# A two-block transformer kernel: the depthwise convolution moves to TensorE, two kinds of narrow products stand in unbroken groups, and the first output projection takes its K-tiles in another order

## The chip, the cores and the metric

The kernel runs on one core of one Trainium2 chip. A core has five engines, each with its own queue of instructions in order: TensorE (PE, with weight loads listed apart as PEld), VectorE (DVE), ScalarE (ACT), GpSimd (POOL) and SyncE (SP), which here issues nearly all DMAs. The metric is device time in microseconds (us), lower is better.

## The reference, cut to what matters

Two blocks work on x of 512 positions by 1024 channels, all in float32. The parts that the change touches:

```python
# first block, mixer: attention over 8 heads of 64, beside a depthwise convolution of 31 taps
q, k, v, f_logit, conv_val, conv_gate = split(h @ w_in)
attn = softmax(q k^T / 8 + cum[t] - cum[s], causal) @ v
u = conv_val * sigmoid(conv_gate)                       # 512 positions x 512 channels
u = sum over d of w[30 - d, c] * u[t - d, c] + b        # 31 taps
u = silu(layer_norm(u))
y = concat([attn, u]) @ w_o                             # K = 1024, then SwiGLU
# second block, state-space mixer: 32 heads of 64, four chunks of 128 positions
y_diag[c] = (scores * exp(seg)) @ xdt                   # 128x128 by 128x64 for each head and chunk
# second block, stick-breaking attention over 16 heads of 64
a = ...;  o = a @ v
```

## The kernel before, in words

The kernel is one program of four stages, *fox* (the first mixer), *ffn*, *mamba* and *sb* (stick-breaking), each with a projection in, its own work and an output projection. Positions are cut into four tiles of 128.

**Projections.** A float32 weight is split into a high part (`whi`, ACT, L268) and a rest (`wlo`, DVE or POOL, L272), and each projection product is three matmuls of 128x512 (L327 to L329). Weights come through a ring of four raw buffers (`load`, L240), which SP fills in the order of a plan (L246). In the plan stand also the tiles of the `ada_w` matrices; DVE sums those up (L498) between other work, and they take the same raw buffers.

**Order of work.** `run` (L184) lays lists of steps beside each other, and a scheduler then sets each engine's order by priorities (the table `PRIO`, L33: a higher number draws a step forward), by dependencies and by its own idea of when an operand is ready. On the chip each engine keeps that order: an instruction that waits holds up all behind it.

**Convolution** (`conv`, L851). A tile `ct` of 128 channels lies with channels in partitions and positions along the row. Tap d adds the row, moved by d, times one weight per channel: one instruction on DVE (L867) for tiles 1 and 2, two (ACT L870, POOL L871) for tiles 3 and 0; tap 0 is an ACT instruction (L865). The table `TAPS` (L52) says how many taps go beside each part of the stage. The taps end during the third attention head pair; then come the layer norm's steps (`ln`, L1025).

**Products with v** (`pv`, L761, used four times in fox and eight times in sb, a pair of heads each time). For each tile s of keys and each head e, the probabilities are transposed (L772), copied from PSUM (L774; ACT for e = 0, DVE for e = 1) and multiplied with v (L780). The product is 64 columns wide; head e writes the half of the PSUM partitions that begins at 64e. A row of the order names a whole product; TensorE runs a float32 product as two instructions, and so the trace counts two for each.

**State-space diagonals** (`diag`, L1262). For each of four groups and four chunks, 16 products of 64x64 (L1267) take the decayed scores that `decay` (L1234, ends with DVE L1244) makes head by head.

**Output projection** (`Out`, L79). `w_o` has eight K-tiles: 0 to 3 are attention's, 4 to 7 the convolution's; they are taken in this order. The last attention pair and the layer norm (L1035) stand between the third and the fourth K-tile.

Of the kernel before, what the change touches and what calls it, by code (L numbers as in the profile page):

```python
# [8 lines left out]
F32 = mybir.dt.float32  # L9
# [7 lines left out]
P = 128  # L17
# [14 lines left out]
NTAP = (30, 30, 0, 0)  # L32
PRIO = {  # L33
    "attend": 15, "attend_last": 190, "ba": 100, "bb": -800, "bc": 200, "bd": 100, "be": 25, "bf": -770, "bl":
    -400, "bn": 90, "bp": -200, "br": -5, "bt": -50, "chain": 100, "colsum": 50, "conv.evac": 20, "conv.fin": 200,
    "conv.split": 0, "conv.sum": -100, "conv.tap": -800, "decay": -860, "erows": 190, "evac": -390, "evac_t": 430,
# [9 lines left out]
    "mamba.sum": -410, "mod": -55, "norm": 50, "off": -10, "osplit": -100, "rows": 200, "sb.evac": 400, "sb.fin":  # L46
# [4 lines left out]

TAPS = (4, 9, 11, 4, 5, 4, 1, 2, 8, 3, 8, 13, 0, 5, 7, 7, 8, 18, 11, 0, 6, 0, 0, 0, 0, 0)  # L52
# [81 lines left out]
class Body:  # L134
# [281 lines left out]
    def consts(self):  # L416
# [25 lines left out]
                                compare_op=ALU.is_ge, fill=0.0)  # L442

# [317 lines left out]
    def pv(self, Ps, v, c0, done, tag="pa"):  # L761

        nc = self.nc
        box, pts = {}, {}

        def trans(s, e):
            if s == 0 and e == 0:
                box["po"] = self.psum(tag)
# [4 lines left out]
            pts[s, e] = self.w512()  # L773
            (nc.scalar.copy, nc.vector.tensor_copy)[e](pts[s, e][:, :N], ps[:, :N])  # L774

        def mms(s):

            for e in (0, 1):
                c = c0 + 64 * e
                nc.tensor.matmul(box["po"][64 * e : 64 * e + 64, s * P :], lhsT=v[:, s, c : c + 64],  # L780
                                 rhs=pts[s, e][:, : S - s * P], start=s == 0, stop=s == NT - 1)

        steps = []
        for i in range(8 + LAG):
            def f(i=i):
                if i < 8:
                    trans(i // 2, i % 2)
                if i >= LAG and (i - LAG) % 2:
                    mms((i - LAG) // 2)
            steps.append(f)  # L790
        return steps + [lambda: done(box["po"])]


    def fox(self):
# [45 lines left out]
        out = Out(self, A["w_o"][0], list(range(8)),  # L840
# [4 lines left out]
        taps, ptaps = [], []  # L845
# [4 lines left out]

        def conv(ct, val, sg):  # L851
            u = us[:, ct, :]
            nc.vector.tensor_tensor(u, val, sg, ALU.mult)  # L853

            def tap(d):
                wc = self.conv_w[:, (30 - d) * 4 + ct : (30 - d) * 4 + ct + 1]
                acc = yc[:, ct, d:]

                def f():
                    with self.prio("tap"):  # L860
                        g()

                def g():
                    if d == 0:
                        nc.scalar.activation(acc, u, AF.Identity, scale=wc, bias=self.v_conv_b[:, ct : ct + 1])  # L865
                    elif d <= NTAP[ct - 1]:
                        nc.vector.scalar_tensor_tensor(acc, u[:, : S - d], wc, acc, ALU.mult, ALU.add)  # L867
                    else:
                        p = self.w512()[:, : S - d]
                        nc.scalar.mul(p, u[:, : S - d], wc)  # L870
                        nc.gpsimd.tensor_tensor(acc, acc, p, ALU.add)  # L871
                return f

            tap(0)()
            return [tap(d) for d in range(1, 31)]

        def some(l, n):
            r, l[:n] = l[:n], []
            return r
# [6 lines left out]
        for k in range(KD):  # L886
            wh, wl = self.take(cu[k])
            self.drop(cu[k])
            if k == KD - 1:
                yc, us = self.big(), self.big()  # L890
                y.append(yc)
# [796 lines left out]
```

## Time and profile before

| | |
|---|---|
| time, three runs | 1434.6, 1439.05, 1439.44 us (median 1439.05) |
| profiled execution | 1434.7 us, span 1432.9 us |
| busy PE, PEld | 1328.3 us (93%), 1024.1 us (71%) |
| busy DVE, ACT, POOL | 953.5 us (67%), 699.6 us (49%), 418.5 us (29%) |
| mean granted TensorE clock | 0.974 of full speed |
| chain that ended last | PE 58%, DVE 18%, issue 7%, POOL 7%, ACT 6%, DMA 2% |

How to read it: busy time is a share of the whole span, but the stages differ. In fox (about the first 300 us) DVE is the fullest engine and PE has gaps; from 340 us on PE is nearly full. The granted clock has two levels, 2.4 GHz (1.0) and 1.2 GHz (0.5); a stretch between them was partly at either. Matmuls overlap, so one matmul's cost is the time from its start to the next one's start, not its listed duration.

### The profile page before, as it was taken

How to read it: one execution, taken by the hardware profiler on the slowest of the kernel's cores; microseconds unless marked ns; L12 is line 12 of the kernel's file. 1: busy time of each engine (PE TensorE's matmuls, PEld its weight loads, DVE VectorE, ACT ScalarE, POOL GpSimd, SP SyncE). 2: the span in 40 equal slices, each digit the busy share in tenths (PEclk: the TensorE clock that was granted, in tenths of full speed). 3: DMA queues.
4: the chain of work that ended last, by engine and by line, in shares of the span. 5: the costliest groups of instructions: out<-in, count | busy, mean ns of one | idle time of the engine just before them, and what ended most of it. 6: DMA issues, size and time to landing. Idle time of an engine off the chain costs nothing.

```text
span 1432.9 us, 19210 instructions
## 1 busy us (share of the span) xinstructions
PE 1328.3 (93%) x7175; PEld 1024.1 (71%) x7175; DVE 953.5 (67%) x1328; ACT 699.6 (49%) x1278; POOL 418.5 (29%) x370
## 2 busy tenths in 40 slices
PE   7895678999999999999899999999999999999897
PEld 5664454777888888888677777787787877566556
DVE  7999998565455454413878978587629428676854
ACT  5463556554222224313768475767426336554633
POOL 3565697214000000000203452544002003353531
PEclk9997799999999999999999999999999999999999
DMA  9553653014376664323357464231243524222101
GB/s 312 163 167 101 204 176 117 21 28 154 120 230 219 191 187 136 96 96 107 88 170 252 145 186 143 86 129 56 74 131 121 175 89 133 61 73 74 59 1 59
DMA packets 126680, 183.76 MB, mean 128 GB/s; under 512 B 8764, under 2 KB 90068, under 8 KB 125564
## 3 DMA queue, kind: packets, MB, share of 16 engines
q1 hardware_dynamic: 126540, 182.54, 40.8%
q8 instruction: 56, 0.92, 0.3%
q14 instruction: 36, 0.29, 0.1%
q10 hardware_dynamic: 48, 0.01, 0.0%
HBM read 174.05 MB, written 2.18 MB: 123 GB/s over the span
## 4 chain that ended last, share of the span: by engine, by line
PE 58%; DVE 18%; issue 7%; POOL 7%; ACT 6%; DMA 2%; SPq 0%; ACTq 0%; DVEq 0%; POOLq 0%
PE pa L329 14%; PE pa L328 13%; PE pa L327 13%; DVE b L867 4%; POOL w L1418 3%; PE ps L328 3%; PE ps L329 3%; PE ps L327 3%; DVE wlo L272 3%; PE pa L780 2%; DVE acc L498 2%; PE ps L772 1%; POOL w L1216 1%; ACT whi L268 1%; DVE w L1416 1%
## 5 line engine op out<-in xcount | busy, mean ns | idle before, releaser
L272 DVE TENSOR_TENSOR wlo<-raw,whi 128x1024 fp32r<-128x1024 f32 (+1 forms) x161 | 208.1, 1303 | 203.6 <-ACT whi L268 202.0
L268 ACT CAST whi<-raw 128x1024 fp32r<-128x1024 f32 (+1 forms) x177 | 183.1, 1046 | 298.1 <-PE pa L328 121.8
L327 PE MATMUL pa<-b,whi 128*128 128x512 f32 x744 | 298.5, 401 | 0.0
L328 PE MATMUL pa<-b,whi 128*128 128x512 f32 x744 | 297.6, 400 | 0.0
L329 PE MATMUL pa<-b,wlo 128*128 128x512 f32 x744 | 297.1, 399 | 0.0
L498 DVE SCALAR_TENSOR_TENSOR acc<-raw,c,acc 128x1024 f32<-128x1024 f32 x84 | 126.3, 1504 | 64.9 <-DMA raw<-in_ada_w_dram 38.9
L327 PE MATMUL pa<-whi,b 128*128 128x512 f32 x424 | 166.8, 395 | 2.8 <-DVE b L853 2.8
L674 POOL TENSOR_TENSOR b<-w,b 128x512 fp32r<-128x512 f32 x24 | 39.3, 1651 | 441.5 <-DVE sm L579 287.8
L329 PEld LDWEIGHTS pa<-b,wlo 128*128 128x128 f32 x744 | 140.7, 189 | 38.4 <-issue 9.5
L328 PE MATMUL pa<-wlo,b 128*128 128x512 f32 x424 | 167.3, 395 | 0.3 <-DVE wlo L272 0.3
L329 PE MATMUL pa<-whi,b 128*128 128x512 f32 x424 | 166.8, 395 | 0.0
L328 PEld LDWEIGHTS pa<-b,whi 128*128 128x128 f32 x744 | 141.4, 190 | 32.6 <-issue 6.1
L327 PEld LDWEIGHTS pa<-b,whi 128*128 128x128 f32 x744 | 140.8, 189 | 31.6 <-issue 4.3
L871 POOL TENSOR_TENSOR b<-b,w 128x511 f32<-128x511 f32 (+29 forms) x60 | 94.1, 1589 | 30.0 <-ACT w L870 28.7
L327 PEld LDWEIGHTS pa<-whi,b 128*128 128x128 f32 x424 | 80.0, 189 | 20.7 <-DVE b L853 4.0
L328 PEld LDWEIGHTS pa<-wlo,b 128*128 128x128 f32 x424 | 80.1, 189 | 17.2 <-DVE wlo L272 1.0
L329 PEld LDWEIGHTS pa<-whi,b 128*128 128x128 f32 x424 | 80.0, 189 | 16.2
L1418 POOL TENSOR_TENSOR w<-w,w 128x127 f32<-128x127 f32 (+3 forms) x64 | 80.8, 1265 | 16.4 <-DVE w L1416 15.2
L772 PE MATMUL ps<-ident,w 128*128 128x128 f32 x240 | 53.2, 295 | 24.3 <-POOL w L1419 12.1
L867 DVE SCALAR_TENSOR_TENSOR b<-b,cw,b 128x511 f32<-128x511 f32 (+29 forms) x60 | 73.4, 1258 | 0.1
L327 PE MATMUL ps<-whi,b 128*128 128x512 f32 x184 | 72.2, 392 | 0.0
L328 PE MATMUL ps<-wlo,b 128*128 128x512 f32 x184 | 72.1, 392 | 0.0
(352 smaller groups left out, 2345.2 us busy)
## 6 DMA issues: line engine op xcount, KB each, us to landing
raw<-in_ada_w_dram SPq DMA_DIRECT2D x80, 512.0 KB, 3.9
raw<-in_w_ffn_in_dram SPq DMA_DIRECT2D x44, 512.0 KB, 4.6
raw<-in_m_in_w_dram SPq DMA_DIRECT2D x40, 512.0 KB, 3.7
raw<-in_w_ffn_out_dram SPq DMA_DIRECT2D x22, 512.0 KB, 4.1
b<-in_ada_w_dram SPq DMA_DIRECT2D x16, 512.0 KB, 7.8
raw<-in_kv_ada_w_dram SPq DMA_DIRECT2D x16, 512.0 KB, 4.8
b<-cumd SPq DMA_DIRECT2D x8, 1024.0 KB, 6.6
raw<-in_m_out_w_dram SPq DMA_DIRECT2D x16, 512.0 KB, 4.4
```

Source lines behind the costliest of these rows:

```text
L268: nc.scalar.copy(hi[:, :n], u.raw)
L272: eng.tensor_tensor(lo[:, :n], u.raw, hi[:, :n].bitcast(F32), ALU.subtract)
L327: mm(ps, lhsT=lh, rhs=rh, start=first, stop=False)
L328: mm(ps, lhsT=lh, rhs=rl, start=False, stop=False)
L329: mm(ps, lhsT=ll, rhs=rh, start=False, stop=last)
L498: nc.vector.scalar_tensor_tensor(acc, raw, ck, acc, ALU.mult, ALU.add)
L674: nc.gpsimd.tensor_tensor(lo, y[i], hi.bitcast(F32), ALU.subtract)
L772: nc.tensor.transpose(ps[:, (t - s) * P : (t - s + 1) * P], Ps()[e][t][:, s * P : (s + 1) * P], self.ident)
L780: nc.tensor.matmul(box["po"][64 * e : 64 * e + 64, s * P :], lhsT=v[:, s, c : c + 64], rhs=pts[s, e][:, : S - s * P], start=s == 0, stop=s ...
L867: nc.vector.scalar_tensor_tensor(acc, u[:, : S - d], wc, acc, ALU.mult, ALU.add)
L871: nc.gpsimd.tensor_tensor(acc, acc, p, ALU.add)
L1418: nc.gpsimd.tensor_tensor(pr_[:, : N - 1], pr_[:, : N - 1], R[:, 1:N], ALU.mult)
```

## The change

Three things are edited.

1. **Convolution.** The tap tables go. `u` of a channel tile is stored to a DRAM tile that has four zeros in front, and loaded back four times, one, two, three and four places moved, into a tile `u4` with 32 channels by 4 moves in the partitions and four channel groups side by side. Products of 128 rows by 32 columns with `taps` (diagonal matrices that POOL makes from the weights) then add up all taps: 8 steps of four moves, four channel groups in four column quarters, so 32 products for a channel tile and 128 in all. The layer norm runs beside the second projection pair. At the start the conv weights are loaded in another layout by eight DMAs, and four DMAs write the zeros.
2. **Groups.** `pv` issues the products of key tiles 0 and 1 as one group and of 2 and 3 as another; `diag` issues a chunk's 16 as one. The first product of a group waits for what the others need as well, and a high priority (3000, also under the names `pv` and `diag_mm` in `PRIO`) keeps a group together.
3. **Output projection of fox.** K-tiles 4 to 7 come first, and the last attention pair runs beside output steps.

```diff
-LAG = 4
+LAG = 2
...
-    -400, "bn": 90, "bp": -200, "br": -5, "bt": -50, "chain": 100, "colsum": 50, "conv.evac": 20, "conv.fin": 200,
+    -400, "bn": 90, "bp": -200, "br": -5, "bt": -50, "chain": 100, "colsum": 50, "conv_mm": 3000, "conv.evac": 20, "conv.fin": 200,
...
+    def wait(self, i, prev):
+        self.tc.add_manual_dep(i, prev.name, mybir.DependencyInfo(
+            mybir.DependencyClass.Sync, mybir.DependencyReason.DATA), reason="wait")
...
     def pv(self, Ps, v, c0, done, tag="pa"):
...
+            if s < 2:
+                pts[s, e] = self.w512()[:, :N]
+            elif e == 0:
+                two = self.w512()
+                pts[s, 0], pts[s, 1] = two[:, :N], two[:, N : 2 * N]
+            copies[s, e] = (nc.scalar.copy, nc.vector.tensor_copy)[e](pts[s, e], ps[:, :N])
+        def mms(*ss):
+            if 0 in ss:
+                box["po"] = self.psum(tag)
+            with self.prio("pv"):
+                for s in ss:
+                    for e in (0, 1):
...
+                        if s == ss[0] and e == 0:
+                            for k in ((s, 1), (ss[1], 0), (ss[1], 1)):
+                                self.wait(m.ins, copies[k].ins)
+        steps = [lambda s=s, e=e: trans(s, e) for s in range(NT) for e in (0, 1)]
+        steps.insert(4 + LAG, lambda: mms(0, 1))
+        return steps + [lambda: None] * LAG + [lambda: mms(2, 3), lambda: done(box["po"])]
...
-        out = Out(self, A["w_o"][0], list(range(8)),
+        out = Out(self, A["w_o"][0], [4, 5, 6, 7, 0, 1, 2, 3],
...
         def conv(ct, val, sg):
+            u = self.w512()
             nc.vector.tensor_tensor(u, val, sg, ALU.mult)
+            nc.sync.dma_start(ud[ct][:, 4:], u)
+            u4 = self.big()
+            loads = [nc.sync.dma_start(u4[32 * s : 32 * s + 32, :, :],
+                                       ud[ct][:, 1 + s : 1 + s + S].rearrange("(g c) x -> c g x", g=4))
+                     for s in range(4)]
+            def products():
+                ps = self.psum()
+                with self.prio("conv_mm"):
+                    for m in range(8):
+                        for g in range(4):
+                            i = nc.tensor.matmul(ps[32 * g : 32 * g + 32, 4 * m :], lhsT=taps[ct // 2][:, ct % 2, 7 - m, g, :],
+                                                 rhs=u4[:, g, : S - 4 * m], start=m == 0, stop=m == 7)
+                            if m == g == 0:
+                                for l in loads:
+                                    self.wait(i.ins, l.ins)
+                nc.scalar.activation(yc[:, ct, :], ps, AF.Identity, bias=self.v_conv_b[:, ct : ct + 1])
...
-        self.run(pv, some(taps, TAPS[2]), some(ptaps, TAPS[3]))
+        self.run(pv[:8])
+        self.run(pv[8:], tp[:3])
...
+            self.run(main[2 * i], self.at("attend", attend(i - 1)) if i else self.at("ln", ln[:6]))
+            self.run(main[2 * i + 1], self.at("scores", scores(i)) + idle, self.at("ln", ln[6:]) if i == 0 else [])
+        self.run(out.steps((0, 1), (0, 1)), self.at("attend_last", attend(2, "ps")))
+        self.run(out.steps((0, 1), (2, 3)), self.at("scores_last", scores(3)) + idle)
+        self.run(out.steps((0, 1), (4, 5)), self.at("attend_last", attend(3, "ps")))
+        self.run(out.steps((2, 3), range(4)))
...
             def diag(c):
...
+                with self.prio("diag_mm"):
...
+                            if i == t == 0 and c == 0:
+                                self.wait(m.ins, box["decayed"].ins)
...
+        for i in range(8):
+            s0 = int(i == 0)
+            nc.sync.dma_start(sw[16 * i : 16 * i + 16, 32 * s0 : P].rearrange("g (s c) -> g s c", c=32),
+                              A["conv_w"][0][4 * i + s0 - 1 : 4 * i + 3, :].rearrange("s (g c) -> g s c", c=32))
+        for u in self.u_pads:
+            nc.sync.dma_start(u, sw[:, P:])
```

On PE in fox, at the end of the value projection, the program before goes from that projection to the gate's 32-column products (L373):

```order
L327 MATMUL pa_991<-whi_968,b_91 128x512
L328 MATMUL pa_991<-wlo_969,b_91 128x512
L329 MATMUL pa_991<-whi_968,b_93 128x512
L373 MATMUL pa_1123<-b_90,whi_999 32x512 x4
L373 MATMUL pa_1123<-b_92,whi_999 32x512 x4
L373 MATMUL pa_1123<-b_91,whi_999 32x512 x4
L373 MATMUL pa_1123<-b_93,whi_999 32x512 x4
```

At the same place the changed program has the convolution's products (L882), of three channel tiles one after the other:

```order
L328 MATMUL pa_989<-whi_1063,b_91 128x512
L329 MATMUL pa_989<-wlo_1064,b_91 128x512
L330 MATMUL pa_989<-whi_1063,b_93 128x512
L473 MATMUL ps_942<-ident,w_888 128x96
L882 MATMUL ps_1014<-b_840,b_872 32x512 x4
L882 MATMUL ps_1014<-b_840,b_872 32x508 x4
L882 MATMUL ps_1014<-b_840,b_872 32x504 x4
L882 MATMUL ps_1014<-b_840,b_872 32x500 x4
```

So 96 products stand ahead of the gate's products there; those of channel tile 0 come right behind them.

On PE in sb, at the first `pv` of that stage, the program before has the products (L780) one or two at a time, between projection matmuls (L327 to L329), transposes (L772) and scores (L749, L754):

```order
L780 MATMUL pa_10244<-w_10250,b_9420 64x512
L328 MATMUL pa_10252<-b_9936,whi_10045 128x512
L780 MATMUL pa_10244<-w_10261,b_9420 64x512
L329 MATMUL pa_10252<-b_9935,wlo_10046 128x512
L327 MATMUL pa_10348<-b_9850,whi_10083 128x512
L772 MATMUL ps_10308<-ident,w_10137 128x128
L328 MATMUL pa_10348<-b_9851,whi_10083 128x512
L780 MATMUL pa_10244<-w_10270,b_9420 64x384
L329 MATMUL pa_10348<-b_9850,wlo_10084 128x512
L749 MATMUL ps_10352<-b_10096 128x128
L780 MATMUL pa_10244<-w_10281,b_9420 64x384
L780 MATMUL pa_10244<-w_10289,b_9420 64x256
```

In the changed program (products L793, transposes L777) the first group stands so:

```order
L777 MATMUL ps_10225<-ident,w_10073 128x128
L329 MATMUL pa_10191<-b_9876,whi_9985 128x512
L777 MATMUL ps_10230<-ident,w_10074 128x128
L777 MATMUL ps_10225<-ident,w_10076 128x128
L793 MATMUL pa_10237<-w_10189,b_9360 64x512
L793 MATMUL pa_10237<-w_10200,b_9360 64x512
L793 MATMUL pa_10237<-w_10209,b_9360 64x384
L793 MATMUL pa_10237<-w_10220,b_9360 64x384
L777 MATMUL ps_10230<-ident,w_10077 128x128
L330 MATMUL pa_10191<-b_9875,wlo_9986 128x512
```

The four products of key tiles 0 and 1 are together and stand ahead of the last transposes; those of tiles 2 and 3 follow as a second group, 11 rows further on.

On SP in fox, the changed program's stores and loads of `u` (L871, L873) stand ahead of the weight loads (L247) that follow the value projection's; the program before has no such rows.

```order
L247 DMA raw_987<-in_ada_w_dram 128x1024
L871 DMA u_95<-w_837 128x512
L467 DMA w_878<-in_conv_ln_g_dram 4x128
L467 DMA w_878<-in_conv_ln_b_dram 4x128
L467 DMA w_878<-in_m_conv_b_dram 24x128
L467 DMA w_878<-in_c_dram 8x128
L873 DMA b_840<-u_95 32x4x512 x4
L871 DMA u_96<-w_849 128x512
```

Each set of four loads waits for its own store; three more such sets follow before SP is past them.

## Rows read from the trace of the kernel before

**Rows 1.** Stretches: us, busy PE, PEld, DVE, ACT, POOL; clock, DMA, GB/s.

```profile
71.40:157.00 85.60, 59.37 (x322) 43.61 (x320) 82.38 (x86) 37.93 (x57) 43.91 (x28) 0.84 0.49 150
157.00:267.00 110.00, 93.96 (x537) 62.05 (x537) 96.88 (x117) 71.11 (x152) 83.49 (x48) 0.92 0.45 139
...
1210.00:1360.00 150.00, 134.58 (x617) 90.28 (x616) 111.33 (x129) 82.37 (x174) 69.92 (x102) 0.98 0.24 67
```

**Rows 2.** Groups by line, 75 to 262 us: count, busy us, mean ns, idle before.

```profile
L867 DVE SCALAR_TENSOR_TENSOR b<-b,cw,b 128x511 f32<-128x511 f32 (+29 forms) x60 | 73.4, 1258 | 0.1
L498 DVE SCALAR_TENSOR_TENSOR acc<-raw,c,acc 128x1024 f32<-128x1024 f32 x20 | 39.0, 1948 | 1.4 <-DMA raw<-in_ada_w_dram 1.4
L871 POOL TENSOR_TENSOR b<-b,w 128x511 f32<-128x511 f32 (+29 forms) x60 | 94.1, 1589 | 30.0 <-ACT w L870 28.7
```

**Rows 3.** Waits, 75 to 262 us: us in total, times, longest.

```profile
PE ps L480 <- DVE acc L498: 16.5, 2, 14.4
PE ps L939 <- DVE w L818: 9.1, 1, 9.1
```

**Rows 4.** Timeline of PE at the gate's 32-column products: start, us.

```profile
102.53 0.39 PE L328 MATMUL pa<-wlo,b 128*128 128x512 f32 x1
102.76 0.39 PE L329 MATMUL pa<-whi,b 128*128 128x512 f32 x1
103.08 3.64 PE L373 MATMUL pa<-b,whi 128*32 128x512 f32 x32
106.65 0.50 PE L327 MATMUL pa<-b,whi 128*128 128x512 f32 x1
```

**Rows 5.** Issues of DMAs by SP in fox: start, us.

```profile
32.72 1.25 SPq L460 DMA_DIRECT2D w<-in_conv_w_dram  x1
...
34.90 1.31 SPq L246 DMA_DIRECT2D raw<-in_w_in_dram  x3
...
88.42 0.39 SPq L246 DMA_DIRECT2D raw<-in_w_in_dram  x1
```

**Rows 6.** DMA issues, 0 to 110 us: count, KB each, us to landing.

```profile
raw<-in_w_in_dram SPq DMA_DIRECT2D x8, 512.0 KB, 3.7
```

**Rows 7.** Timeline of PE over one `pv` of sb.

```profile
1247.41 1.07 PE L780 MATMUL pa<-w,b 128*64 128x512 f32 x2
1248.42 0.50 PE L328 MATMUL pa<-b,whi 128*128 128x512 f32 x1
...
1250.86 0.86 PE L780 MATMUL pa<-w,b 128*64 128x384 f32 x2
1251.65 0.50 PE L329 MATMUL pa<-b,wlo 128*128 128x512 f32 x1
...
1252.14 0.86 PE L780 MATMUL pa<-w,b 128*64 128x384 f32 x4
1252.93 0.33 PE L754 MATMUL ps<-b,b 128*128 128x128 f32 x1
1253.18 0.86 PE L780 MATMUL pa<-w,b 128*64 128x256 f32 x6
1253.98 0.50 PE L327 MATMUL pa<-b,whi 128*128 128x512 f32 x1
```

**Rows 8.** Timeline of PE at the last `pv` of fox.

```profile
264.68 2.37 PE L780 MATMUL ps<-w,b 128*64 128x512 f32 x14
266.98 0.50 PE L327 MATMUL pa<-b,b 128*128 128x512 f32 x1
```

**Rows 9.** DVE groups in sb, 1224 to 1348 us.

```profile
L272 DVE TENSOR_TENSOR wlo<-raw,whi 128x1024 fp32r<-128x1024 f32 x11 | 17.6, 1596 | 0.1
L774 DVE COPY w<-ps 128x128 f32<-128x128 f32 (+3 forms) x21 | 9.9, 478 | 24.1 <-PE ps L772 24.1
```

**Rows 10.** The diagonal products over the whole span, by form.

```profile
L1267 PE MATMUL ps<-w,b 128*64 128x64 f32 x512 | 23.2, 228 | 0.7 <-DVE b L1244 0.7
```

**Rows 11.** Timeline of PE at one chunk's diagonals in an unbroken run.

```profile
859.50 1.15 PE L1267 MATMUL ps<-w,b 128*64 128x64 f32 x32
860.58 0.50 PE L327 MATMUL pa<-b,whi 128*128 128x512 f32 x1
```

More of the change, by code (lines that the diff above doesn't have):

```diff
@@ L763, in pv @@
         nc = self.nc
[L764 removed]
+        box, pts, copies = {}, {}, {}
         def trans(s, e):
[L767 to L768 removed]
             N = S - s * P
@@ L772, in trans @@
                 nc.tensor.transpose(ps[:, (t - s) * P : (t - s + 1) * P], Ps()[e][t][:, s * P : (s + 1) * P], self.ident)
[L773 to L791, printed above, removed]
+            if s < 2:
[10 more added lines that the diff above has]
+                    for e in (0, 1):
+                        c = c0 + 64 * e
+                        m = nc.tensor.matmul(box["po"][64 * e : 64 * e + 64, s * P :], lhsT=v[:, s, c : c + 64],
+                                             rhs=pts[s, e], start=s == 0, stop=s == NT - 1)
+                        if s == ss[0] and e == 0:
[4 more added lines that the diff above has]
+        return steps + [lambda: None] * LAG + [lambda: mms(2, 3), lambda: done(box["po"])]
     def fox(self):
@@ L849, in sigmoid @@
             return sg
+        ud = [self.dram.tile([P, S + 4], F32, name=f"u{ct}", tag=f"u{ct}") for ct in range(4)]
+        taps = []
         def conv(ct, val, sg):
-            u = us[:, ct, :]
+            u = self.w512()
             nc.vector.tensor_tensor(u, val, sg, ALU.mult)
[L855 to L872, printed above, removed]
@@ new lines, in conv, with diagonals @@
+            return products
+        def diagonals():
+            w4 = self.conv_w.rearrange("p (m t g) -> p m t g", m=8, t=4)
+            for i in range(2):
+                taps.append(self.big().rearrange("p a b -> p (a b)").rearrange("p (t m g c) -> p t m g c", t=2, m=8, g=4))
+                for t in range(2):
+                    nc.gpsimd.tensor_tensor(taps[i][:, t], w4[:, :, 2 * i + t, :].unsqueeze(3).to_broadcast([P, 8, 4, 32]),
+                                            self.E4.unsqueeze(1).unsqueeze(1).to_broadcast([P, 8, 4, 32]), ALU.mult)
@@ L917, in fox @@
         n = len(self.instructions())
-        taps += [t for z in zip(*tp[:2]) for t in z]
-        ptaps += tp[2]
         self.stage = "conv"
+        diagonals()
         vectors = self.vectors()
-        self.run(c3, some(taps, TAPS[0]), some(ptaps, TAPS[1]))
+        self.run(c3)
         self.behind(n, m)
         vectors()
-        tp = conv(0, got["val"], sg)
-        ptaps[:] = [t for z in zip_longest(ptaps, tp) for t in z if t]
+        tp.append(conv(0, got["val"], sg))
         self.stage = "fox"
         v.append(self.big())
-        self.run(pv, some(taps, TAPS[2]), some(ptaps, TAPS[3]))
+        self.run(pv[:8])
+        self.run(pv[8:], tp[:3])
         self.run(pf)
```

60 lines of the change are left out of this document (28 added, 32 removed).

## The prediction

> **What bounds the kernel now.** I read the busy shares by stretch first, then the groups by line in the fullest stretch, then the waits there, and last the timeline of PE around the instructions that the change regroups.
>
> The stretches [rows 1] cut fox at two places: from the first matmul behind the start's products (71.4 us) to the end of the sums over the gates (157 us), and from there to the end of the last attention pair (267 us). In both DVE is the full engine: 82.38 of 85.60 us and 96.88 of 110.00 us. PE is busy 59.37 and 93.96 us, so it idles 26.2 and 16.0 us, and its granted clock is 0.84 and 0.92 on average: part of the time it runs at 1.2 GHz instead of 2.4, behind the gaps. From 340 us on PE is full; what is taken from it there is gained nearly one for one. In sb it idles 15.4 of 150 us (the 1210 to 1360 stretch).
>
> The groups [rows 2] say what fills DVE: 60 taps of the convolution, 73.4 us, then 39.0 us of `ada_w` sums. POOL carries 94.1 us of taps too. The waits [rows 3] say what PE waits for: 16.5 us for a DVE sum, 9.1 us for DVE's chain of small operations on the gates. Both stand in DVE's queue among taps.
>
> **The change part by part.** The sum is made against the profiled execution, 1434.7 us (span 1432.9 and 1.8 around it).
>
> *The taps leave.* DVE's load over the two stretches falls from 179.3 to 105.9 us, POOL's by 94 us, and neither is near full afterwards. What is late next is PE, with its new products.
>
> *The convolution on PE.* 32 products for each of four channel tiles, in quads whose four products write different quarters of the PSUM partitions. The gate's products have the same shape: 16 float32 products of 128 rows, 32 columns and N = 512, so four quads. They take from 103.08 to 106.65 [rows 4], 3.57 us, 0.89 a quad; a projection matmul beside them takes 0.23 from start to start, 0.32 where the shape changes. The new products are 484 to 512 long, 498 on average: 0.89 x 498 / 512 = 0.87, and 32 quads make 27.8 us. The order lets three channel tiles run into each other for a few rows, where two products want the same quarter in turn; I add 0.8 for that and the shape changes, 28.6 in all. The bounds are 27.8 and, if no two products ran together, 128 times the lone narrow product of [rows 7] (1.01 us, 64 columns), 126 us; the row of the same shape decides for 28.6.
>
> The Trainium skill (TensorE: Matmul & The Clock Gate, Part 3, Packing small matmuls) gives a measured 2.38 times for three column tiles of 32, so 0.79 for each; four at that rate would be 3.2 times. As an estimate from that page and the lone product, the convolution would be 126 / 3.2 = 39 us and the forecast 11 us higher. The trace does not agree: its quads run faster than that, and they decide.
>
> *First stretch.* Counting the two orders up to the end of the sums over the gates, 197 projection matmuls become 163, 34 x 0.23 = 7.8 us less; the others come later. PE's busy time goes from 59.4 to 59.4 - 7.8 + 28.6 = 80.2. About 5 of the 59.4 are the doubled durations at 1.2 GHz; with PE dense I take 4 of them back: 76. Of the idle 26.2 us, the sum that PE waited for is no longer behind taps, and the gate chain has about 37 projection matmuls (8 us) as cover. I keep 3. The stretch becomes 79 against 85.6.
>
> Behind a conv product that waits stands all of PE's queue. SP stores u, then waits for the store before the four loads, for one channel tile after the other. A weight load of 512 KB lands 3.7 us after issue [rows 6]; u's store is half of it, a set of loads twice. With 3.7 for each of the two, and 2 us of issues, a tile takes 7 to 9 us, from about 79 us on, when the second tile's gate is done (estimate): three tiles are in by 100 to 106, and their products begin at about 100 and need 7 us each. Tile 0's come 10 us later. I price this wait at nothing; if a round trip took double, the second and third tile's products would wait some 8 us each. The weights for the first query projection stand behind these loads in SP's queue and are issued at about 104 us instead of 88.42 [rows 5]; PE then still has the conv products of one tile and the gate's ahead of them, and wants them some 20 us later.
>
> *Second stretch.* 189 projection matmuls instead of 142 stand before its end, 47 x 0.23 = 10.8 more. Four `pv` calls are shorter by 2 each (below), 8 less. Of about 7.5 us that the low clock costs here (94.0 x 0.08), I take 3.5 back. Busy: 94.0 + 10.8 - 8 - 3.5 = 93.3. Of the idle 16 us I keep 11: each pair's softmax still makes PE wait, and in the new order the first pair has 18 transposes in a row without any filler. So 104 against 110.0. The two stretches together lose 6.6 + 5.7 = 12.3 us, and the 13 matmuls more (352 against 339) that are done by then are worth 3.0: fox gains 15. Its bounds are 0, if another wait takes the place of the taps, and 38, if all the idle time but 3 us goes and the clock stays at 2.4 GHz.
>
> *Groups in `pv`.* One call of sb [rows 7]: the first product of N = 512 takes 1.01 us before a projection matmul can start, and so does the second, which stands apart; then 0.79, 0.79 and 0.80 us for the rest. That is 4.4 us, and each of the five runs costs 0.2 more for the change of shape in and out (0.32 and 0.33 instead of 0.23 from start to start): 5.4. The last call of fox happened to run almost whole: 14 of the 16 instructions in 2.30 us [rows 8], the other two apart. So a whole call is about 2.3, with two groups 2.7. A call gains 2.7, eight calls 21.4. Against it stands the new wait: a group's first product needs the copy of the last transpose, only three transposes and a matmul earlier. A copy takes 0.48 us on DVE, and a weight split in front of it 1.60 [rows 9]. The wait is between 0 and 2.1; I take 0.4, the copy's own length less the cover, as no split stands there most times. sb gains 21.4 - 3.2 = 18, with ends 5 and 21.
>
> *Groups in `diag`.* 512 instructions are 23.2 us of busy time [rows 10] in 36 separate runs; with 0.2 for each run's two shape changes they cost 29 from start to start. A whole chunk takes 1.08 us [rows 11]; 16 chunks with their shape changes are 20.5. The difference is 8.5. The four groups that now wait for a last decay take something back, between 0 and 2 us each; PE waited 0.7 us in all for this cause so far. I take 0.9 each: mamba gains 5.
>
> *The output projection's order* costs nothing by itself: the layer norm now ends some 60 us before the first output product, and the last attention pair has output products beside it. That is in the second stretch.
>
> *The start.* Two DMAs that take SP from 32.72 to 34.90 [rows 5] become twelve, eight with pieces of 128 bytes and four with 16. At the 1.09 us of these rows the added ten would take 11 us, at the 0.4 of the lightest three below them 4. The weights behind them on SP land 3.7 us after their issue [rows 6], and are split on ACT and DVE before PE can use them. I take most of the delay as hidden by the buffers issued before it; if that cover is gone it costs about 6, near the middle of 4 and 11. I take 1.
>
> The Trainium skill (DMA: Bandwidth & Descriptors, Specifications) says that transfers below 512 bytes go by read-modify-write, which speaks against both layouts. No row here shows such a transfer. By it the start would sit at its upper end and the sum be 5 us higher.
>
> Sum: -15 - 18 - 5 + 1 = -37, so 1434.7 - 37 = 1397.7 against the profiled execution. That was the fastest of the times shown with one run (1434.6); the other two lie 4.4 above. I leave the sum where it is and say 1398.
>
> **The rivals.**
>
> *A. The new waits eat the groups' gain.* Each first group waits 2.1 us in sb, 1.7 more than I took, 13.4 for eight, and the four diagonal groups lose 1 more each: 1398 + 17 = 1415. For it: PE keeps its order, and DVE carries scans and splits there. Against it: all four copies but the last are long done.
>
> *B. Fox stays where it is.* Another wait takes the place of the taps: the chain on the gates, the `ada_w` sums (39.0 us on DVE, fed by a ring that PE's weights share), or the softmax of each pair. Then fox gains nothing and the time is 1413. For it: DVE's sums took 1.95 us each. Against: DVE is left with 106 us of work in 180.
>
> *C. Slower: the round trips starve PE.* The conv products stand at the head of PE's queue with everything behind them, and the weights behind u's loads on SP. If a round trip takes 20 us instead of 8, four of them cost 48 us: 1398 + 48 = 1446. It passes the time before from about 17 us a trip. For it: four dependent store and load pairs on one queue. Against: the 3.7 us that a larger load takes.
>
> *D. Fox gains all it can.* PE is dense at 2.4 GHz and fox gains 35: 1378.
>
> *E. The regrouped products don't run side by side* and the convolution costs 126 us. The quads of [rows 4] all but exclude it.
>
> **How the numbers follow.** My forecast (1398, its own range 1387 to 1409) has 0.48, A 0.12, B 0.16, C 0.05, D 0.18, E 0.01. The range that holds eight in ten takes in D, B and A and leaves out C: 1372 to 1418. Within 0.5% (7 us) is about what a measurement of this kernel can't tell from no change. All cases but C and E are faster by more; with something kept for A and B together with a dear start, the chances are 0.90 faster, 0.05 the same, 0.05 slower.
>
> **What would show it.** In the profile after: no tap on DVE or POOL; 27 to 30 us from start to start on the conv products and no wait over 2 us at their first; DVE busy under 70% between 71 us and the last attention pair, and that stretch at 175 to 185 us; the groups of `pv` at about 1.5 and 0.8 us with waits under 0.5; each chunk's diagonals at 1.1 us; the clock over 0.98. I am wrong if PE idles more than 20 us in fox, if its first conv product waits for a DMA, or if `pv` and `diag` shorten PE's work and sb and mamba don't get shorter.

## The result and the profile after

The changed kernel takes 1419.62 us (median of four runs, 1414.52 to 1422.12), the kernel before beside it 1436.82: the ratio is 0.9876, 95% interval 0.9839 to 0.9913. So it is faster, by 17.2 us, where 37 were forecast; the time lies 1.6 us above the range. The profiled execution took 1422.1 us, the upper end of the four; against the profiled execution of the kernel before (1434.7 us) it gains 12.6, and that is what the table below divides up.

To see where the time went I count the 4464 projection matmuls of either kernel in the order of their starts (the 128x512 triples, number 0 to 4463) and compare when the same number starts. The length of a stretch less PE's busy time in it is PE's idle time. "Low clock" is half of PE's busy time in the pieces at 1.2 GHz, so that their work is counted as at 2.4 GHz; "work" is the busy time that remains. A second execution of the changed kernel (in the experiments) is shown beside the first, because they differ.

| stretch, by matmul number | before, us | after | change | again | forecast |
|---|---|---|---|---|---|
| start, to 0 | 71.4 | 77.5 | +6.1 | +5.2 | +1 |
| fox, 0 to 540 | 256.1 | 249.6 | -6.5 | -12.3 | -15 |
| ffn, 540 to 2000 | 342.9 | 338.3 | -4.6 | -2.5 | 0 |
| mamba, 2000 to 3200 | 351.1 | 357.3 | +6.2 | +6.7 | -5 |
| to 4000 | 197.2 | 197.1 | -0.1 | -0.4 | 0 |
| sb, 4000 to the end | 205.8 | 192.4 | -13.4 | -12.6 | -18 |

The rows behind it are those of the stretches, as in [rows 1]: us, busy PE, PEld, DVE, ACT, POOL, then the granted clock, DMA share and GB/s. Of the kernel before, for fox, mamba and sb:

```profile
71.40:327.50 256.10, 208.66 (x1139) 150.16 (x1138) 214.94 (x294) 142.56 (x285) 143.76 (x85) 0.90 0.39 118
670.40:1021.50 351.10, 337.81 (x2098) 264.95 (x2097) 276.51 (x443) 235.55 (x447) 119.67 (x100) 1.00 0.42 132
1218.70:1424.50 205.80, 188.91 (x857) 129.71 (x855) 139.86 (x180) 99.22 (x216) 78.46 (x116) 0.98 0.18 54
```

Of the changed kernel:

```profile
77.50:327.10 249.60, 226.68 (x1394) 157.11 (x1394) 143.45 (x235) 110.02 (x227) 62.32 (x30) 0.94 0.47 137
665.40:1022.70 357.30, 334.52 (x2098) 264.63 (x2098) 280.14 (x443) 235.75 (x447) 112.03 (x100) 1.00 0.41 130
1219.80:1412.20 192.40, 174.98 (x855) 129.34 (x856) 137.43 (x180) 96.86 (x216) 80.72 (x116) 0.96 0.20 58
```

In fox DVE's busy time falls from 214.94 to 143.45 us and PE's idle time from 47.4 to 22.9; PE's own work rises by 21. In mamba PE is busy 3.3 us less and idle 9.5 us more (13.3 to 22.8), so the stage gets longer though PE has less to do. In sb nearly all of the change is PE's busy time.

The convolution does what the quads of [rows 4] said. The timeline of PE in the changed kernel (start, us, as there):

```profile
107.88 0.30 PE L473 MATMUL ps<-ident,w 96*128 96x96 f32 x1 [2.19 <-DMA w<-in_kv_norm_g_dram]
108.11 20.29 PE L882 MATMUL ps<-b,b 128*32 128x512 f32 x192
128.18 3.66 PE L374 MATMUL pa<-b,whi 128*32 128x512 f32 x32
...
133.00 6.89 PE L882 MATMUL ps<-b,b 128*32 128x512 f32 x64
```

The products take 20.1 us for three channel tiles and 6.8 for the last, 26.9 in all (28.6 forecast). None waits for the loads of u. The one wait there, 2.19 us, is for a small load of a vector that now stands among those of u on SP. The longest waits of PE from 77.5 to 254.1 us are these (us in total, times, longest), beside [rows 3]:

```profile
PE ps L958 <- DVE w L828: 5.1, 1, 5.1
PE ps L777 <- ACT w L984: 3.2, 2, 2.7
PE ps L487 <- POOL w L1025: 2.6, 1, 2.6
```

The `ada_w` sum that PE awaited for 16.5 us makes it wait no more. The 2.6 us are at the same helper line, but for another sum, the layer norm's sum of squares on POOL (L1025). The chain on the gates still costs 5.1.

In sb, the products with v before and after (one group of instructions each: count, busy us, mean ns, idle before; these are seven of the eight calls, the last writes a tile of another name), then one call of the changed kernel as the timeline shows it, beside [rows 7]:

```profile
L780 PE MATMUL pa<-w,b 128*64 128x512 f32 (+3 forms) x112 | 32.8, 456 | 0.0
```

```profile
L793 PE MATMUL pa<-w,b 128*64 128x512 f32 (+3 forms) x112 | 17.9, 443 | 1.3 <-ACT w L783 1.1
```

```profile
1245.78 1.72 PE L793 MATMUL pa<-w,b 128*64 128x512 f32 x8
...
1250.25 0.87 PE L793 MATMUL pa<-w,b 128*64 128x256 f32 x8 [0.19 <-ACT w L783]
```

A call is 1.66 and 0.80 us from start to start. The waits for copies come to 1.3 us over all eight calls; 3.2 was forecast.

In mamba all sixteen chunks of diagonals are unbroken, each 1.08 us where nothing is waited for, as [rows 11] showed. The waits are where the gain went. PE's waits in mamba before (655 to 1022 us), the two largest on head-group work:

```profile
PE ps L328 <- POOL w L1216: 5.1, 6, 1.5
...
PE ps L327 <- ACT w L1215: 1.6, 4, 0.5
```

And in the changed kernel (L1231, L1232 are the same two lines of `parts`, which splits an operand of the state products):

```profile
PE ps L329 <- POOL w L1232: 4.7, 8, 1.4
PE ps L328 <- ACT w L1231: 4.6, 6, 1.2
...
PE ps L1284 <- issue: 1.6, 1, 1.6
PE pa L328 <- ACT b L90: 1.5, 1, 1.5
PE ps L1284 <- DVE w L1269: 1.4, 1, 1.4
PE ps L1336 <- DVE b L1330: 1.3, 1, 1.3
```

The wait for the last decay (L1260 here), the only new one that I priced, stands among them as "issue". The group that PE starts at 853.38 us begins 0.10 us after DVE has ended the last decay, which stands behind a weight split and an `ada_w` sum:

```profile
851.40 1.28 DVE L505 SCALAR_TENSOR_TENSOR acc<-raw,c,acc 128x1024 f32<-128x1024 f32 x1
852.60 0.68 DVE L1260 TENSOR_TENSOR b<-b,w 128x512 f32<-128x512 f32 x1
```

```profile
853.38 1.15 PE L1284 MATMUL ps<-w,b 128*64 128x64 f32 x32 [1.59 <-issue]
```

The group at 985.74 us begins 0.10 us after its last decay too, with 0.36 us of waiting, so this cause takes 2.0 us in all. The rest of the 9.5 stands elsewhere: at the state products, at the output projection's split of its activations (L90), at `xs`'s product on DVE (L1269) and at the last transposes (L1336).

### The profile page after: what moved, and what is told of

Read it like the earlier page. It is cut to its first block, busy times and chain, and to the rows that moved or that the text cites. A ratio compares the mean times of both kernels' runs of the same rounds, so it can differ in the third digit from the quotient of the medians.

```text
span 1420.4 us, 19562 instructions
## 1 busy us (share of the span) xinstructions
PE 1329.8 (94%) x7431; PEld 1030.8 (73%) x7431; DVE 882.9 (62%) x1268; ACT 668.1 (47%) x1224; POOL 329.1 (23%) x321
## 4 chain that ended last, share of the span: by engine, by line
PE 54%; DVE 10%; POOL 8%; ACT 8%; issue 7%; DMA 2%; POOLq 0%; ACTq 0%; DVEq 0%
PE pa L329 13%; PE pa L328 13%; PE pa L330 13%; POOL w L1437 4%; PE ps L329 3%; PE ps L330 3%; PE ps L328 3%; ACT whi L269 2%; POOL w L1232 2%; DVE wlo L273 2%; PE ps L777 1%; PE pa L793 1%; ACT b L1258 1%; DMA raw<-in_ada_w_dram 1%; DVE w L1435 1%
## 5 line engine op out<-in xcount | busy, mean ns | idle before, releaser
L273 DVE TENSOR_TENSOR wlo<-raw,whi 128x1024 fp32r<-128x1024 f32 (+1 forms) x161 | 213.8, 1338 | 221.1 <-ACT whi L269 218.8
L329 PE MATMUL pa<-b,whi 128*128 128x512 f32 x744 | 297.7, 400 | 0.0
L329 PE MATMUL pa<-wlo,b 128*128 128x512 f32 x424 | 168.0, 397 | 1.4 <-DVE wlo L273 1.4
L505 DVE SCALAR_TENSOR_TENSOR acc<-raw,c,acc 128x1024 f32<-128x1024 f32 x84 | 117.8, 1403 | 79.4 <-DMA raw<-in_ada_w_dram 55.4
L329 PEld LDWEIGHTS pa<-b,whi 128*128 128x128 f32 x744 | 141.9, 191 | 28.6 <-issue 2.0
L681 POOL TENSOR_TENSOR b<-w,b 128x512 fp32r<-128x512 f32 x24 | 36.0, 1518 | 469.7 <-DVE sm L586 288.1
L329 PEld LDWEIGHTS pa<-wlo,b 128*128 128x128 f32 x424 | 80.6, 190 | 18.5 <-DVE wlo L273 2.1
L777 PE MATMUL ps<-ident,w 128*128 128x128 f32 x240 | 55.9, 307 | 23.5 <-POOL w L1438 13.3
L328 PE MATMUL ps<-whi,b 128*128 128x512 f32 x184 | 72.3, 393 | 0.0
L329 PE MATMUL ps<-wlo,b 128*128 128x512 f32 x184 | 72.1, 392 | 0.0
L330 PE MATMUL ps<-whi,b 128*128 128x512 f32 x184 | 71.9, 391 | 0.0
L777 PEld LDWEIGHTS ps<-ident,w 128*128 128x128 f32 x240 | 33.5, 152 | 45.3 <-POOL w L1438 17.4
```

Source lines behind the costliest of these rows:

```text
L273: eng.tensor_tensor(lo[:, :n], u.raw, hi[:, :n].bitcast(F32), ALU.subtract)
L328: mm(ps, lhsT=lh, rhs=rh, start=first, stop=False)
L329: mm(ps, lhsT=lh, rhs=rl, start=False, stop=False)
L330: mm(ps, lhsT=ll, rhs=rh, start=False, stop=last)
L505: nc.vector.scalar_tensor_tensor(acc, raw, ck, acc, ALU.mult, ALU.add)
L681: nc.gpsimd.tensor_tensor(lo, y[i], hi.bitcast(F32), ALU.subtract)
```

## The experiments

Times are medians; each ratio is to the kernel before in the same comparison, with its 95% interval.

**The changed kernel again.** No edit.

> The changed kernel once more, as it is, to see how far one profile differs from the next. Stages by the start of the same projection matmul (number 0, 540, 2000, 3200 and the last): before 71.4, 327.5, 670.4, 1021.5 us; after 77.5, 327.1, 665.4, 1022.7. If the order of instructions makes the losses (both theories below), the start comes again at 77 to 78 us, fox takes 249 to 251 us, the stretch from number 2000 to 3200 takes 355 to 358 us (before 351.1). If the losses were chance, 71 to 74 us and 349 to 352 us. Time 1414 to 1423 us.

1417.83 us, 0.9885 (0.9868 to 0.9902). The losses in the start and in mamba come again within 1 us, as they would if they lay in the order of the instructions. Fox differs by 5.8 us (243.8 against 249.6, where 249 to 251 was expected): low clock cost 13.1 us in one execution and 6.7 in the other, with the same idle time, 22.9.

**Diagonals as before in the changed kernel.**

```diff
-                with self.prio("diag_mm"):
                     for i in range(8):
...
-                            if i == t == 0 and c == 0:
-                                self.wait(m.ins, box["decayed"].ins)
```

> The changed kernel with the state-space diagonals issued as before, without their priority and without the wait. Theory 'the groups make PE wait': PE's idle time between projection matmuls number 2000 and 3200 goes from 22.8 back to about 13 us while PE's own work there rises by 5, so the stretch takes 351 us instead of 357 and the kernel 1413 to 1416. Rival 'something else in the new program delays mamba (where the stage falls, its loads, the clock)': the idle time stays at 20 us or more, the work rises by 5, and the kernel gets slower by 3 to 5 us, 1422 or more.

1414.38 us, 0.9861 (0.9843 to 0.9879). The stretch of mamba:

```profile
662.30:1016.80 354.50, 339.61 (x2098) 265.99 (x2097) 277.81 (x443) 235.47 (x447) 118.19 (x100) 1.00 0.42 131
```

Work rises from 332.7 to 337.9 us, idle time falls from 22.8 to 14.9: the stretch is 2.8 us shorter than with the groups (351 was expected, 1.7 us of low clock fell into it). The rival falls. The interval of the whole time overlaps with that of the changed kernel, so the stretch shows it better than the time. Over the four profiles of the changed program with all the groups (its two executions, and below the later loads and the row behind the sum) and the four without any (this one, and below the convolution alone, `combo` and `combo_late`) the stretch takes 357.0 and 353.0 us on average, with 22.3 and 13.2 us of idle time, 332.6 and 337.7 of work and 2.1 of low clock in both. So the groups cost about 4 us there; what is left of the 6.2 is low clock, which comes with them and without.

**The groups of diagonals without the added wait.**

```diff
-                            if i == t == 0 and c == 0:
-                                self.wait(m.ins, box["decayed"].ins)
```

> The changed kernel with the priority of the diagonals kept, but without the added wait of each first product for the last decay. If the wait is what costs, PE's idle time between projection matmuls number 2000 and 3200 falls from 22.8 to 13 to 15 us and the time to about 1413. If it is the priority (a group drawn forward, with others behind it), the idle time stays at 20 to 23 us and the time at 1419.

1415.66 us, 0.9866 (0.9851 to 0.9881); mamba 356.8 us.

```profile
659.80:1016.60 356.80, 339.42 (x2098) 264.27 (x2097) 281.10 (x442) 236.50 (x447) 115.77 (x100) 1.00 0.42 130
```

Neither theory is borne out: idle time falls to 17.4 us, but without the wait the products of the first chunks come apart again (27 runs in the timeline instead of 16), and the work is back at 337.7. Whether the wait or the priority costs more stays open.

**The groups of diagonals alone, in the kernel before.** The edit is the part of the diff in `decay` and `diag`, with `diag_mm` in `PRIO`.

> The kernel before with the groups of the state-space diagonals alone. Theory 'the groups take more idle time than they save work': between projection matmuls number 2000 and 3200 (before 351.1 us) PE's work falls by 5, its idle time rises by 8, the stretch takes 353 to 356 us, and the kernel is 2 to 5 us slower than before, 1437 to 1440. Rival 'it costs only beside the other two edits': the stretch takes 346 to 348 us and the kernel 1430 to 1432.

1438.45 us, 1.0033 (1.0015 to 1.0052): slower than the kernel before. Mamba:

```profile
668.50:1026.30 357.80, 337.46 (x2097) 267.12 (x2097) 279.39 (x443) 235.53 (x447) 110.84 (x100) 0.99 0.41 130
```

Work falls by 5.4 us, to 332.4, idle time rises by 7.0, to 20.3, and low clock takes 5.1 where it took none. The rival falls: this part loses by itself, 3.8 us of the whole time and 6.7 in that stretch, a little more than expected. Without the low clock of this one execution the stretch loses 1.6.

**Groups for the first three head groups only.** The last one has fewer projection matmuls beside it.

```diff
-                with self.prio("diag_mm"):
+                with self.prio("diag_mm" if g < 3 else "none"):
...
-                            if i == t == 0 and c == 0:
+                            if i == t == 0 and c == 0 and g < 3:
```

> The changed kernel with the diagonals of the last of the four head groups issued as before, those of the first three in groups. Theory 'the groups lose where the products of other work run out, in the last head group': PE's idle time between projection matmuls number 2000 and 3200 falls from 22 to 16 to 17.5 us, its work rises by 0 to 1.5 from 332.5, the stretch takes 350 to 353 us instead of 357.5 and the kernel 1411 to 1414. Rival 'each head group loses its part': the stretch takes 355 to 357 us and the kernel 1416 to 1418.

1416.66 us, 0.9870 (0.9843 to 0.9898), as the rival has it; mamba 354.3 us, between the two. Idle time falls by 2.9 us, to 19.9, and work rises by 1.7; the rest of the 3.0 is low clock, 1.7 us with all the groups and none here. So about a third of the added idle time is in the last head group, where the changed kernel's timeline has three waits that the kernel before has not,

```profile
993.32 0.50 PE L328 MATMUL pa<-whi,b 128*128 128x512 f32 x1 [1.45 <-ACT b L90]
...
998.25 1.93 PE L1284 MATMUL ps<-w,b 128*64 128x64 f32 x32 [1.44 <-DVE w L1269]
...
1012.88 0.30 PE L1336 MATMUL ps<-ident,b 128*128 128x128 f32 x1 [1.28 <-DVE b L1330]
```

and the rest is in the other three. My theory that other work runs out only at the end falls.

**The groups of `pv` alone, in the kernel before.** The edit is `pv`, `wait`, `LAG` and `pv` in `PRIO`.

> The kernel before with the groups of pv alone (the products with v, their copies' waits, priority 3000). Theory 'the forecast over-priced the switches, the clock took some back': from projection matmul number 4000 to the last (before 205.8 us) PE's own work falls by 17, idle time stays within 1 of 16.9, and the stretch takes 191 to 194 us; the kernel takes 1419 to 1424, as the four calls of fox save 0 to 3 us beside DVE. Rival 'the groups are worth 21 and the loss in sb comes from the rest of the change': the stretch takes 187 to 189 us.

1428.97 us, 0.9961 (0.9945 to 0.9977). Fox, then sb:

```profile
70.90:331.10 260.20, 205.21 (x1139) 150.34 (x1138) 214.65 (x294) 142.97 (x285) 145.85 (x85) 0.89 0.38 117
1222.90:1415.90 193.00, 174.65 (x855) 129.53 (x856) 138.13 (x180) 97.08 (x216) 80.23 (x116) 0.96 0.19 58
```

sb is 12.8 us shorter: work falls by 17.6, idle time rises by 1.4, low clock by 3.4. The forecast of 18 was too high in itself. The time expected was missed: fox did not gain 0 to 3 us, it lost 4 in this profile. There the groups save PE 6.3 us of work, and beside a full DVE (214.65 us) PE idles 7.5 us more.

**Convolution and output order alone.** The changed kernel with `pv` and `diag` of before.

> The changed kernel with pv and the diagonals as before: what is left is the convolution on TensorE and the other order of the output projection. Theory 'fox gains 9 to 11 us from the first projection matmul on and the start loses 5': number 0 comes at 75 to 78 us, number 540 at 323 to 329 (before 327.5), the kernel takes 1429 to 1434. Rival 'the convolution gains all that fox gained and more, and the groups of pv cost there': number 540 at 318 to 321, the kernel 1424 to 1427.

1431.95 us, 0.9980 (0.9963 to 0.9997), with a spread of 1426 to 1441. The profiled execution is the slowest of ten (1441.15 us), and its number 540 comes at 336.7 us, later than either theory has it. In its fox idle time is 25.6 us, 22 less than before, and work 220.1, 28 more: the stretch is 260.1 us against 256.1. So the convolution moves PE from waiting to working and gains little alone. The saving by `pv` in fox is 6.6 us of work here against the changed kernel. By the medians the groups of `pv` alone gain 5.7 us, this part alone 2.8, and the two together (the changed kernel with its diagonals as before) 20.5, so 12 us come only when both are there. That the reason is DVE, full without the convolution's part, is argued from the waits of one profile each.

**The weights of the convolution loaded later.**

```diff
-        for i in range(8):
...
+        def conv_loads():
+            for i in range(8):
...
             if k == 1:
                 self.ada_raw(KD - 1)
+            if k == 2:
+                self.conv_loads()
```

> The changed kernel with the eight loads of the convolution's weights and the four stores of zeros issued behind the ring's load of the third K-tile of the start, not ahead of it. Theory 'SP's queue delays the start': SP issues the first weights of that group at about 35 us instead of 41.82, the first projection matmul behind the start comes at 71 to 73 us instead of 77.5 and the kernel takes 1413 to 1415. Rival 'the delay is the new work on DVE and POOL at the start, or the order there': it stays at 76 to 78 us and the time at 1419.

1418.45 us, 0.9892 (0.9874 to 0.9909). SP issues the ring's weights at 34.68 us; in the changed kernel they are late, as the timeline of SP shows, and ACT waits for them:

```profile
34.33 5.49 SPq L1530 DMA_DIRECT2D w<-in_conv_w_dram  x8
39.94 1.78 SPq L1533 DMA_DIRECT2D u<-w  x4
41.82 1.33 SPq L247 DMA_DIRECT2D raw<-in_w_in_dram  x3
```

```profile
45.69 0.94 ACT L269 CAST whi<-raw 128x896 fp32r<-128x896 f32 x1 [2.83 <-DMA raw<-in_w_in_dram]
```

That wait of ACT is gone with the later loads. But number 0 still comes at 75.3 us and PE's idle time ahead of it, counted from 2 us on, stays at 13.5 us, as in the changed kernel: the rival holds for most of the delay.

**A sum's first row behind the start's last column sum.** In the changed kernel one instruction on DVE (L503, the first of an `ada_w` sum) stands inside the last column sum of the start (L1605, L1607), on which the last K-tile waits. DVE and POOL in the changed kernel:

```profile
62.65 1.00 DVE L1605 SCALAR_TENSOR_TENSOR w<-b,c,w 128x256 f32<-128x256 f32 x2
64.45 1.15 DVE L503 TENSOR_SCALAR acc<-raw,c 128x1024 f32<-128x1024 f32 x1 [0.81 <-DMA raw<-in_ada_w_dram]
65.53 2.29 DVE L1605 SCALAR_TENSOR_TENSOR w<-b,c,w 128x256 f32<-128x256 f32 x1
67.93 0.43 DVE L1607 TENSOR_TENSOR w<-w,w 128x256 f32<-128x256 f32 x1
```

```profile
65.02 2.52 POOL L273 TENSOR_TENSOR wlo<-raw,whi 128x896 fp32r<-128x896 f32 x1
```

The row waits 0.81 us for its raw buffer and takes 1.15, and the step behind it, 0.50 us elsewhere, takes 2.29 beside POOL's split. PE waits 2.59. The edit:

```diff
+                    if self.last_col is not None:
+                        self.order(i.ins, self.last_col)
```

> The changed kernel with the first row of an ada_w sum ordered behind the start's last column sum on DVE, where the kernel before has it; nothing else is moved by hand. Theory 'this row in front of the last column sum costs the start 2.6 to 2.9 us': PE's wait of 2.6 us there goes, PE's idle time up to projection matmul number 0 falls from 13.5 to 10.5 to 11.5, number 0 comes at 72 to 74 us instead of 76.6, and the kernel takes 1414 to 1416. Rival 'DVE is late anyway (the sum only fills a wait)': the idle time stays at 13 or more and number 0 at 75 to 77 us.

1417.08 us, 0.9881 (0.9866 to 0.9896). The steps are unbroken:

```profile
61.67 1.52 DVE L1609 SCALAR_TENSOR_TENSOR w<-b,c,w 128x256 f32<-128x256 f32 x3
63.30 1.33 DVE L1611 TENSOR_TENSOR w<-w,w 128x256 f32<-128x256 f32 x1
```

PE's idle time up to number 0 falls from 13.5 to 10.7 us and number 0 comes at 72.3. In each of the seven executions with the row in front PE waits 2.6 us at that place, in none of the four with the row behind. So the row is the cause of 2.6 of the 3.6 us of idle time that the start gained; the rest of its 5 to 6 us is mostly low clock (1.5 to 3.2 us more than before). But the time hardly moved (1414 to 1416 was expected): number 540 comes at 322.0 us. The six executions with the row in front that have both the convolution and the groups of `pv` have it at 320.3 to 327.1, 322.0 on average. What the start gives back, fox takes (249.7 us). Low clock alone is no cause, at 11.4 us it is within the 6.7 to 13.1 of the others. The waits point at DVE's product for u (L874 here), which projection matmuls wait for:

```profile
PE pa L329 <- DVE w L874: 2.2, 2, 1.4
```

In the six executions with the row in front this wait takes 0 to 0.7 us, in the four with it behind (this one and the three below) 1.6 to 3.8, and idle time in fox is 21.8 and 24.1 us on average. No run was made to show that it is the cause.

**Combined.** `combo` has the diagonals as before and the row behind the column sum, `combo_first3` the groups of the first three head groups instead, `combo_late` is `combo` with the later loads.

> The changed kernel with all diagonals as before and the row of the ada_w sum behind the start's last column sum. If the two add: number 0 at 72 to 73 us (76.6 in the changed kernel), the stretch from number 2000 to 3200 at 353 to 355 us, the kernel 1410 to 1414. If the start's gain is given back in fox (another wait is late there): number 540 at 320 to 322 as in the changed kernel, the kernel 1414 to 1415.

> The changed kernel with the last head group's diagonals as before and the row of the ada_w sum behind the start's last column sum: the two losses of the changed kernel mended and the groups kept where they cost nothing. If both add: number 0 at 72 to 73 us, the stretch from number 2000 to 3200 at 350 to 353 us, the kernel 1407 to 1412, the fastest of all. If the start's gain is given back: 1411 to 1414.

> The changed kernel with all three losses mended: the diagonals as before, the row of the ada_w sum behind the start's last column sum, and the loads of the convolution's weights behind the ring's load of the third K-tile. If SP's queue has a part of its own in the start (ACT waits 2.2 to 4.0 us for a raw buffer at about 45 us in the changed kernel, and PE 2.7 to 3.8 at about 54 in some executions): no such wait of PE, number 0 at 70.5 to 72 us, the kernel 1410 to 1413. Rival 'the wait for the buffer is hidden each time': number 0 at 72.5 to 76 and the kernel at 1413 to 1415 as without the late loads.

1413.43 us (0.9841, 0.9819 to 0.9864), 1414.51 (0.9858, 0.9832 to 0.9884) and 1412.33 (0.9843, 0.9819 to 0.9867). The last is the fastest of all medians, though its interval doesn't part it from `combo`. Its mamba is back where it was before the change:

```profile
662.10:1013.20 351.10, 337.87 (x2098) 264.86 (x2097) 276.36 (x443) 235.56 (x447) 118.88 (x100) 1.00 0.42 132
```

`combo` has the numbers expected if the two gains add (number 0 at 72.8 us, the stretch of mamba at 353.4), but its time isn't parted from that of the diagonals as before alone (0.9861). In the three, number 0 comes at 72.8, 76.0 and 73.8 us and number 540 at 318.5, 324.2 and 323.8, 322.2 on average: past fox nothing is left of the start's gain. `combo_first3` missed what was expected of it in all three numbers: its mamba took 355.8 us, no 350 to 353. `combo_late` has the time of the theory and the number 0 of its rival. SP's queue has its own part in the start: with the loads in the old place PE waits 0.3 to 0.5 us at 51 to 55 us in five executions and 2.7 to 3.8 in four, with the later loads in neither of two. It is hidden at times, not each time.

## Why the prediction was too low

**The step that failed is the one on `diag`: "I take 0.9 each: mamba gains 5."** It lost 6.2 to 6.7. Three parts make up the 11 us between. The first is the work saved, over-priced at 8.5: it is 5.1 to 5.4. The price of 0.2 us for a run's changes of shape was about twice too high, and it was put on busy times in which neighbours overlap (23.2 us; from start to start the 36 runs take 20.8, the 16 chunks 17.3, which leaves 0.1 us for each of the 20 runs fewer). As recorded, 23.2 and 36 times 0.2 make 30.4 and not 29. The second is the waits. I looked only at the new one, for the last decay, and priced it at 3.6 us; it takes 2.0. But idle time rises by 7 to 9.5 us (the kernel before with this part alone, and the changed kernel), for the neighbours wait too. The products in pieces had been standing in PE's queue between the state products, the splits and the transposes; they are now in blocks of 32. The third is low clock, 1.7 to 3.4 us, which the other runs show with and without the groups. That the groups lose is shown by taking them out and by putting them in alone. That it is the loss of work to fill with, rather than the changed order in some other respect, is argued from the places of the waits; the three runs that cut the groups differently didn't isolate it. Rival A had the right kind of loss at the wrong place: in mamba its price was 4 us of waiting more than mine, at the last decay, and 5.9 more came, at others; its price in sb was 13.4, and there nothing like it came.

**Up to the end of fox, 5.5 us gained on average (327.5 to 322.0) where 14 were forecast.** The mechanism was right: the taps leave, the quads run side by side, DVE is no longer full, SP gets from one store of u to the next in 7.7 to 8.1 us, as forecast, and PE never waits for them. Of fox's own 15 us, 6.5 came in one execution and 12.3 in the other. PE's work rose by 21.1 and 21.8 us, close to the 20.6 of the sum (28.6 less 8). Its idle time is 22.9 us where the sum leaves 19.2 (3, 11, and the 5.2 that stood behind the second stretch already). The miss is in the first stretch, 7.3 instead of 3: 5.1 at the gate chain, which I took as covered, and 2.2 at the small load among those of u. The clock gave back 3.1 us in one execution and 9.5 in the other where I took 7.5; that the sum comes near with the second is luck. The start was "1, up to 6" and cost 5 to 6, half of it for a reason that I had not listed, a row moved on DVE; since number 540 stands still when it is mended, it can't be added to fox. Rival B, fox gaining nothing, is nearer in size than the forecast, but not in cause: the `ada_w` sums and the gate chain cost PE 5.1 us in place of 25.6.

**sb gained 13.4 of 18.** The wait at the groups was over-priced (1.3 us instead of 3.2), the saving too: work fell by 17.4, not 21.4. With the runs' own time (33.9 us before, 19.5 after, from the timelines) there are 3.0 us left for 22 runs fewer, so a run's two changes of shape cost 0.14 us together rather than 0.2. And the clock took 3.4 us back: 17.1 us of that stretch are at 1.2 GHz, 9.6 in the kernel before.

**ffn gained 2.5 to 4.6 us** that I had not counted: PE's waits behind its first transposes went from 2.9 us to between 0 and 1.9, and low clock from 1.6 to 0.

Rivals C, D and E fell: no trip was late, fox kept 22.9 us of idle time, and the products ran four abreast. Two of the signs of being wrong came: PE idles more than 20 us in fox, and mamba didn't get shorter though PE's work there did. The estimate from the Trainium skill (TensorE: Matmul & The Clock Gate, Part 3, Packing small matmuls), 39 us, was 12 us too high; 26.9 was measured. The twelve small DMAs of the start take SP's queue 7.3 us of issue where two took 2.2: 5.1 added, within the 4 to 11 forecast. No wait in the trace is for their landing, so it doesn't show what the Trainium skill (DMA: Bandwidth & Descriptors, Specifications) says of transfers below 512 bytes.

## What to carry to other kernels

Narrow products in a queue between other work aren't only a cost of shape changes: they can be what the engine does while their neighbours' operands come. Grouping them paid in sb, where idle time rose by 0.5 us, and lost in mamba, where it rose by 9.5; that they were the filling there is the reading that fits, not one that a run shows. Price a regrouping by the waits of its neighbours as well as by its own new wait, and read in the order what else a planner has moved.

## What the hardware showed

- A float32 product with 64 columns and N = 512 costs 1.0 us alone; the four products of two key tiles, 3.6 us in the pieces of [rows 7], take 1.66 in a group. Four of 32 columns run abreast (0.84 us for each four, N = 484 to 512).
- A DVE step with two operands in SBUF took 2.29 us instead of 0.50 while POOL's split ran from 65.02 to 67.54 (one case). The Trainium skill (SBUF — State Buffer, SBUF: two separate sides) has the two engines sharing a port pair under an exclusive lock; the rows agree, as the step ended 0.28 us after the split.
- The same program's clock differs between executions: in fox low clock cost 13.1 us in one execution of the changed kernel and 6.7 in the other, and between these in its eight variants that keep the convolution and the groups of `pv`. A change of 5 us there can't be read from one profile.
